# RWKV-7 scan of a hybrid trunk: the identity product of the state, cut to 64 rows and issued behind U

## The chip, the cores and the metric

The kernel runs on one core of a Trainium2 chip. The metric is the device time of one execution in microseconds (us), the median of several runs. An execution that the hardware profiler recorded comes with it; all durations of single instructions below are from that one execution.

## The reference

A trunk of four layers over 512 latent tokens and 256 context tokens, 1024 wide: a convolution module, a bidirectional RWKV-7 mixer, attention, a second convolution module. The change lies in the RWKV-7 layer, in the scan over tokens. Each of the 16 heads keeps a state S of 64 x 64, and for each token

```python
sa  = einsum("bhvk,bhk->bhv", S, -kk_t)
S   = S * d_t[:, :, None, :] + sa[..., None] * (kk_t * a_t)[:, :, None, :] + v_t[..., None] * k_t[:, :, None, :]
out = einsum("bhvk,bhk->bhv", S, r_t)
```

It runs once forwards and once backwards over the tokens, and the two outputs are added.

## The kernel before, in words

The scan works on chunks of 64 tokens (C = 64), so that a chunk is a few small matrix products in place of 64 steps. The 16 heads are taken in eight pairs; a pair p fills the 128 partitions, head 0 on partitions 0 to 63 (slice A), head 1 on 64 to 127 (slice B). There are 12 chunks, so 12 steps i for each pair and direction d. A **round** below is one pair p with its 12 steps; there are eight rounds, one after the other.

One step of one direction, `scan` (lines 1330 to 1389), is a generator that is advanced in six pieces. The tile VT holds, for each head, the state or U on the head's own 64 partitions and the values of the chunk on the other 64.

1. Line 1350, the **c products**: `pc[own, 0] = GM^T VT`, one product for each head, with all 128 rows of VT. Behind it, line 1354, the **identity products** `pS[own] = ident[:, hc]^T VT`: 128 rows by 64 columns, of which the 64 rows of the other half meet zeros in the identity. They put the old state into the PSUM half pS, for the sum of line 1373. They stand in the steps 1 to 10 of a round (`0 < i < 11`).
2. ACT copies the c product to **Z** (line 1093 by way of `cpy`).
3. Line 1361, the **R S products** into the half pO of the same bank (own state times R, 64 x 64), and line 1364, the **U products** `pc[own, 1] = Tt^T Z` (64 x 64).
4. ACT copies U into VT, one copy for each head (**U copies**, `cpy("U", ...)`, line 1093). They overwrite the old state in VT.
5. Line 1370 adds U and values to pO; line 1373 adds them to pS.
6. ACT scales pS into the VT of the next chunk (**state copies**, line 1378), and ACT (line 1093) or DVE (line 1385) takes pO into the output O.

pO and pS are two halves of one PSUM bank, tile `o0` or `o1` by direction, one buffer each. So the first product that writes the tile in a step must wait until ACT or DVE has read the tile of the step before; in the steps 1 to 10 that is the identity product of line 1354.

The order on PE, ACT, DVE and GpSimd is the order in which the code issues. The two directions alternate, d = 0 and then d = 1 for each piece, and between the pieces a list of events (`side`, `stream`) issues the work of other stages: the features of the next quarters (pz line 1116, pc line 1126; DVE's sg line 1122 stands between them), the Gram matrices (pg line 1166, masked by DVE in line 1170), turns (pt line 1192), the values of the next pair (pv line 1231), the triangular inverse of the next pair (DVE, tm line 1269 and Ti line 1272, in turn), its 64-wide part (px lines 1301 and 1314) and the centring of the last pair's output (gm line 1400). In the last round the gate's projection (line 189) fills the places between the pieces instead.

A matmul of 32-bit floats appears in the profile as two records, so the two heads' products of one direction, called a **pair of products** here, are four records ("x4").

Of the kernel before, what the change touches and what calls it, by code (L numbers as in the profile page):

```python
# [45 lines left out]
    A=[64.18, 65.3143, 66.1364, 69.4498, 69.7397, 70.3889],  # L46
    B=[2.44, 4.09473, 7.27024, 8.71365, 9.3943, 9.83957],
# [31 lines left out]
class Trunk:  # L79
# [952 lines left out]
    def rwkv_scan(self, i, rk, cv, vproj):  # L1032
        nc, tc, I = self.nc, self.tc, self.I
# [29 lines left out]
        ident = self.ident  # L1063
        self.mask3 = self.mask.rearrange("p (g c) -> p g c", c=C).unsqueeze(1).to_broadcast([P, 3, 2, C])
        A, B = slice(0, 64), slice(64, 128)
# [24 lines left out]
        def cpy(key, k, out, in_):  # L1090
            e = OPT["E"][key][k]
            if e == "a":
                nc.scalar.activation(out, in_, AF.Copy)  # L1093
            elif e == "d":
                nc.vector.tensor_copy(out, in_)
            else:
                nc.gpsimd.tensor_scalar(out=out, in0=in_, scalar1=1.0, scalar2=0.0, op0=ALU.mult, op1=ALU.add)
# [235 lines left out]
        def scan(p, d, G):  # L1333


            if d == 0:
                G["O"] = late["s"].tile([P, TOK], F32, tag="O", name="O", bufs=2)
            O, Tt = G["O"], G["Tt"]
            for i in range(12):
                h, q = divmod(i, NQ)  # L1340
                assert (p, h) in vdone and (p, h, d) in gdone and (p, h) in idone
                VT, GM, AR, BKT = (G["VT", h], *(G[n, h, d] for n in ("GM", "AR", "BKT")))
                dc = G["DC", h, d][:, q:q + 1]
                hc = lambda hd: slice(hd * C, (hd + 1) * C)
                pc = late["c"][d][:, 0:2 * C].rearrange("p (n c) -> p n c", c=C)
                po = late["p"].tile([P, 2 * C], F32, tag=f"o{d}", name=f"o{d}")
                pO, pS = po[:, 0:C], po[:, C:]
                for hd, own, oth in ((0, A, B), (1, B, A)):
                    rows = oth if i == 0 else slice(0, P)
                    nc.tensor.matmul(pc[own, 0, :], GM[rows, 2 * hd, q, :], VT[rows, d, q, hc(hd)], start=True, stop=True)  # L1350

                if 0 < i < 11:
                    for hd, own in ((0, A), (1, B)):
                        nc.tensor.matmul(pS[own], ident[:, hc(hd)], VT[:, d, q, hc(hd)], start=True, stop=False)
                yield
                Z = late["s"].tile([P, C], F32, tag=f"Z{d}", name="Z", bufs=1)
                cpy("Z", d, Z, pc[:, 0, :])
                yield
                if i:
                    for hd, own in ((0, A), (1, B)):  # L1360
                        nc.tensor.matmul(pO[own], VT[own, d, q, hc(hd)], AR[own, 1, q, :], start=i == 11, stop=False)
                tu = (h * 2 + d) * NQ + q
                for own in (A, B):
                    nc.tensor.matmul(pc[own, 1, :], Tt[own, tu, :], Z[own], start=True, stop=True)  # L1364
                yield
                cpy("U", 2 * d, VT[A, d, q, 0:C], pc[A, 1, :])
                cpy("U", 2 * d + 1, VT[B, d, q, C:2 * C], pc[B, 1, :])
                yield
                for hd, own in ((0, A), (1, B)):
                    nc.tensor.matmul(pO[own], VT[:, d, q, hc(hd)], GM[:, 2 * hd + 1, q, :], start=i == 0, stop=i == 11)  # L1370
                if i < 11:
                    for hd, own in ((0, A), (1, B)):
                        nc.tensor.matmul(pS[own], BKT[:, q, hc(hd)], VT[:, d, q, hc(hd)], start=False, stop=True)  # L1373
                yield
                if i < 11:
                    h2, q2 = divmod(i + 1, NQ)
                    for hd, own in ((0, A), (1, B)):
                        nc.scalar.activation(G["VT", h2][own, d, q2, hc(hd)], pS[own], AF.Copy, scale=dc[own])  # L1378

                c0 = (i if d == 0 else (3 - i if i < 4 else 15 - i)) * C  # L1380
                oc = O[:, c0:c0 + C] if d == 0 else O[:, c0:c0 + C][:, ::-1]
                if i in (0, 1, 4, 5, 6, 7):
                    cpy("O", d, oc, pO)
                else:
                    nc.vector.tensor_tensor(out=oc, in0=pO, in1=oc, op=ALU.add)
                if i == 11:
                    sdone.add((p, d))
                yield
# [93 lines left out]
        with ExitStack() as man:  # L1482
# [11 lines left out]
            for w in range(6):  # L1494
                ev = next(X)
                for n in range(18):
                    v_steps(18 * w + n)
                    for t, g in ev:
                        if n <= t < n + 1:
                            next(g)  # L1500
            chain = {p: [named(scan(p, d, GS[p]), f"scan{p}") for d in range(2)] for p in range(NT)}
            for p in range(-1, NT + 1):
                ev = side(p)
# [590 lines left out]
```

## Time and profile before

| | us |
|---|---|
| median of 3 runs | 2457.43 (2450.3 to 2457.45) |
| the profiled execution's own time | 2465.75 |
| its span from first to last instruction | 2464.0 |
| its first and last c product (line 1350) start at | 870.5 and 1404.8 |
| stretch 870 to 1410: PE, DVE, ACT busy | 486, 330, 357 of 540 |

In the timeline a row is a start, a length, an engine, a line with its operation, output and inputs, and in brackets the time that the engine stood idle before it and what ended that; an idle time below about 0.16 us is not shown. PE's records overlap, since matmuls are pipelined: the distance from start to start is what a product takes of PE, and the length contains its way through the array.

### The profile page before, as it was taken

How to read it: one execution, taken by the hardware profiler on the slowest of the kernel's cores; microseconds unless marked ns; L12 is line 12 of the kernel's file. 1: busy time of each engine (PE TensorE's matmuls, PEld its weight loads, DVE VectorE, ACT ScalarE, POOL GpSimd, SP SyncE). 2: the span in 40 equal slices, each digit the busy share in tenths (PEclk: the TensorE clock that was granted, in tenths of full speed). 3: DMA queues.
4: the chain of work that ended last, by engine and by line, in shares of the span. 5: the costliest groups of instructions: out<-in, count | busy, mean ns of one | idle time of the engine just before them, and what ended most of it. 6: DMA issues, size and time to landing. Idle time of an engine off the chain costs nothing. (4 is left out here: it accounts for less than half of the span.)

```text
span 2464.0 us, 45546 instructions
## 1 busy us (share of the span) xinstructions
PE 2252.8 (91%) x17855; PEld 1785.8 (72%) x17855; DVE 1445.3 (59%) x2597; ACT 1102.4 (45%) x2642; POOL 509.8 (21%) x600
## 2 busy tenths in 40 slices
PE   7999978899988798898988999888999999989987
PEld 4677757577666677777766678887999889865545
DVE  4787774734463766666664343546455464667664
ACT  4222243324542266666667543456455454432232
POOL 0000002000101232232210014544454444410000
PEclk8999989998989889899898999999999999989999
DMA  8787633365665644444434381111111211314442
GB/s 273 229 239 216 176 105 120 108 211 171 190 177 183 175 115 118 106 120 124 116 77 127 122 242 52 53 35 52 52 52 52 61 61 52 95 26 131 122 125 81
DMA packets 358897, 304.41 MB, mean 124 GB/s; under 512 B 110755, under 2 KB 300315, under 8 KB 358683
## 3 DMA queue, kind: packets, MB, share of 16 engines
q1 hardware_dynamic: 358683, 301.51, 42.3%
q8 instruction: 141, 2.31, 0.4%
q14 instruction: 73, 0.60, 0.1%
HBM read 215.82 MB, written 57.77 MB: 111 GB/s over the span
## 5 line engine op out<-in xcount | busy, mean ns | idle before, releaser
L176 ACT ACTIVATE whi<-wraw 128x1024 fp32r<-128x1024 f32 x168 | 177.0, 1056 | 383.9 <-PE cps L189 157.9
L374 DVE SCALAR_TENSOR_TENSOR Y<-yp,VC,Y 128x783 f32<-128x783 f32 (+1 forms) x256 | 229.2, 908 | 7.7 <-ACT Y L367 3.1
L178 DVE TENSOR_TENSOR wlo<-wraw,whi 128x1024 fp32r<-128x1024 f32 x98 | 120.4, 1229 | 175.7 <-ACT whi L176 175.7
L178 POOL TENSOR_TENSOR wlo<-wraw,whi 128x1024 fp32r<-128x1024 f32 x70 | 168.3, 2407 | 186.3 <-ACT whi L176 178.2
L1847 PE MATMUL pj<-whi,hhi 128*128 128x256 f32 x640 | 181.9, 285 | 5.2 <-ACT junk L1856 3.6
L189 PE MATMUL cps<-hhi,whi 128*128 128x512 f32 x576 | 179.3, 367 | 2.9 <-ACT hhi L288 2.9
L1847 PE MATMUL pj<-wlo,hhi 128*128 128x256 f32 x640 | 181.3, 284 | 0.0
L1847 PE MATMUL pj<-whi,hlo 128*128 128x256 f32 x640 | 181.2, 284 | 0.0
L189 PE MATMUL cps<-hlo,whi 128*128 128x512 f32 (+1 forms) x576 | 176.3, 360 | 0.0
L189 PE MATMUL cps<-hhi,wlo 128*128 128x512 f32 x576 | 176.0, 360 | 0.0
L189 PEld LDWEIGHTS cps<-hhi,whi 128*128 128x128 f32 x576 | 96.4, 190 | 48.3 <-issue 18.6
L1847 PEld LDWEIGHTS pj<-whi,hhi 128*128 128x128 f32 x640 | 123.1, 192 | 6.5 <-ACT junk L1856 4.2
L189 PE MATMUL ops<-hhi,whi 128*128 128x512 f32 (+1 forms) x320 | 104.5, 368 | 24.7 <-ACT hhi L449 22.4
L1847 PEld LDWEIGHTS pj<-wlo,hhi 128*128 128x128 f32 x640 | 123.2, 193 | 0.7
L1847 PEld LDWEIGHTS pj<-whi,hlo 128*128 128x128 f32 x640 | 122.8, 192 | 0.1
L1378 ACT ACTIVATE VT<-o,DC 64x64 f32<-64x64 f32 x352 | 108.5, 308 | 26.7 <-PE o L1373 17.2
L189 PEld LDWEIGHTS cps<-hlo,whi 128*128 128x128 f32 x576 | 96.2, 189 | 28.3 <-issue 10.1
L189 PEld LDWEIGHTS cps<-hhi,wlo 128*128 128x128 f32 x576 | 95.5, 189 | 24.1 <-issue 6.7
L189 PE MATMUL ops<-hhi,wlo 128*128 128x512 f32 (+1 forms) x320 | 106.7, 364 | 3.0 <-POOL wlo L178 2.2
L1093 ACT ACTIVATE VT<-c 64x64 f32<-64x64 f32 x384 | 83.5, 217 | 57.7 <-PE c L1364 49.5
L189 PE MATMUL ops<-hlo,whi 128*128 128x512 f32 (+1 forms) x320 | 105.0, 357 | 0.0
L1272 DVE TENSOR_TENSOR Ti<-Ti,tm 96x31 f32<-96x31 f32 (+15 forms) x248 | 99.7, 402 | 7.3 <-POOL tm L1269 1.3
(347 smaller groups left out, 5717.6 us busy)
## 6 DMA issues: line engine op xcount, KB each, us to landing
mraw<-in_mod_w_dram SPq DMA_DIRECT2D x36, 1024.0 KB
wraw<-in_conv_w_in_dram SPq DMA_DIRECT2D x48, 512.0 KB
wraw<-in_attn_w_in_dram SPq DMA_DIRECT2D x48, 512.0 KB
X<-yp SPq DMA_DIRECT2D x128, 98.9 KB
mraw<-in_mod_w_dram SPq DMA_DIRECT2D x24, 512.0 KB
KR<-dF SPq DMA_DIRECT2D x24, 384.0 KB
F<-dF SPq DMA_DIRECT2D x24, 384.0 KB
X<-yp SPq DMA_DIRECT2D x128, 65.5 KB
```

The source lines that it names most:

```text
L176: nc.scalar.activation(hi[:, :n], raw[:, :n], AF.Copy)
L178: lo_eng.tensor_tensor(out=lo[:, :n], in0=raw[:, :n], in1=hi.bitcast(F32)[:, :n], op=ALU.subtract)
L189: nc.tensor.matmul(ps, a[:, k, m0:m0 + m], b[k0 + k][:, ts], start=first and k == 0 and i == 0, stop=last and k == kt - 1 and i == 2)
L374: taps.append(lambda v=v: nc.vector.scalar_tensor_tensor(out=Y[m], in0=y[:, pe + v:pe + v + nout], scalar=self.vec("dw", nv)[:, v * NT + m ...
L1093: nc.scalar.activation(out, in_, AF.Copy)
L1272: eng("ia", j).tensor_tensor(out=Ti[0:96, j + 1:32, 0:c], in0=Ti[0:96, j + 1:32, 0:c], in1=o, op=ALU.add)
L1378: nc.scalar.activation(G["VT", h2][own, d, q2, hc(hd)], pS[own], AF.Copy, scale=dc[own])
L1847: nc.tensor.matmul(o[:, n, :], a, b[:, k, :], start=kh == 0 and k == 0 and e == 0 and n == 0, stop=kh == 1 and k == 3 and e == 2 and n == 1)
```

## The change

The identity products move from behind the c products to behind the U products, and use only the 64 rows of the head's own half: `ident[own, hc]` and `VT[own, ...]` in place of all 128 rows. So they are 64 x 64 products in a group of 64 x 64 products. In the steps 1 to 10 the R S product of line 1361 (1358 after the change) now writes the bank first and opens it (`start=True`), and the identity product adds with `start=False`. What is computed is the same, and so is the number of products: 20 pairs of products in a round.

```diff
                     nc.tensor.matmul(pc[own, 0, :], GM[rows, 2 * hd, q, :], VT[rows, d, q, hc(hd)], start=True, stop=True)
-
-                if 0 < i < 11:
-                    for hd, own in ((0, A), (1, B)):
-                        nc.tensor.matmul(pS[own], ident[:, hc(hd)], VT[:, d, q, hc(hd)], start=True, stop=False)
                 yield
                 Z = late["s"].tile([P, C], F32, tag=f"Z{d}", name="Z", bufs=1)
                 cpy("Z", d, Z, pc[:, 0, :])
                 yield
+
                 if i:
                     for hd, own in ((0, A), (1, B)):
-                        nc.tensor.matmul(pO[own], VT[own, d, q, hc(hd)], AR[own, 1, q, :], start=i == 11, stop=False)
+                        nc.tensor.matmul(pO[own], VT[own, d, q, hc(hd)], AR[own, 1, q, :], start=True, stop=False)
                 tu = (h * 2 + d) * NQ + q
                 for own in (A, B):
                     nc.tensor.matmul(pc[own, 1, :], Tt[own, tu, :], Z[own], start=True, stop=True)
+                if 0 < i < 11:
+                    for hd, own in ((0, A), (1, B)):
+                        nc.tensor.matmul(pS[own], ident[own, hc(hd)], VT[own, d, q, hc(hd)], start=False, stop=False)
                 yield
                 cpy("U", 2 * d, VT[A, d, q, 0:C], pc[A, 1, :])
```

PE's order in step 10 of a round, before (c is the tile of Z and U, o that of output and state, each with one number for each direction; `o<-VT,C` is the identity product, since C holds the identity; px and pt are work of other stages):

```order
L1350 MATMUL c_6692<-VT,GM 64x64 x2
L1354 MATMUL o_10002<-VT,C 64x64 x2
L1350 MATMUL c_6693<-VT,GM 64x64 x2
L1354 MATMUL o_10009<-VT,C 64x64 x2
L1301 MATMUL px<-TP,LO 32x32 x24
L1361 MATMUL o_10002<-AR,VT 64x64 x2
L1364 MATMUL c_6692<-Z,Tt 64x64 x2
L1361 MATMUL o_10009<-AR,VT 64x64 x2
L1364 MATMUL c_6693<-Z,Tt 64x64 x2
L1192 MATMUL pt<-C,BK 128x128 x3
```

PE's order at the same place after the change (lines 1358, 1361 and 1364 are now the R S, the U and the identity products):

```order
L1350 MATMUL c_6692<-VT,GM 64x64 x2
L1350 MATMUL c_6693<-VT,GM 64x64 x2
L1301 MATMUL px<-TP,LO 32x32 x24
L1358 MATMUL o_10002<-AR,VT 64x64 x2
L1361 MATMUL c_6692<-Z,Tt 64x64 x2
L1364 MATMUL o_10002<-VT,C 64x64 x2
L1358 MATMUL o_10007<-AR,VT 64x64 x2
L1361 MATMUL c_6693<-Z,Tt 64x64 x2
L1364 MATMUL o_10007<-VT,C 64x64 x2
L1192 MATMUL pt<-C,BK 128x128 x3
```

Two pairs of products have gone from ahead of px, one of them from between the two directions' c products, to a place ahead of pt, each right behind its direction's U products. The neighbours of both groups are the same as before.

ACT's order with its waits, before, at step 2 of a round (the four `VT<-c` are the U copies, two for each direction; `waits PE` is a wait for a product):

```order
L1093 ACTIVATE BKT<-pt 128x384
L1130 ACTIVATE Dt<-pc 128x6x64 [waits PE_49,Pool_49]
L1093 ACTIVATE VT<-c_6692 64x64 [waits PE_49,Activation_49]
L1093 ACTIVATE VT<-c_6692 64x64 [waits Activation_49]
L1093 ACTIVATE VT<-c_6693 64x64 [waits PE_49,Activation_49]
L1093 ACTIVATE VT<-c_6693 64x64 [waits Activation_49]
L1378 ACTIVATE VT<-o_12481,DC 64x64 [waits PE_49]
```

ACT's order at the same place after the change:

```order
L1093 ACTIVATE BKT<-pt 128x384
L1130 ACTIVATE Dt<-pc 128x6x64 [waits PE_49,Pool_49]
L1093 ACTIVATE VT<-c_6692 64x64 [waits PE_49,Activation_49] x2
L1093 ACTIVATE VT<-c_6693 64x64 [waits PE_49,Activation_49] x2
L1378 ACTIVATE VT<-o_12481,DC 64x64 [waits PE_49]
```

The order on ACT is the same, but each U copy now has its own wait for PE. A U copy overwrites the state that the identity product reads, and that product now stands behind the U product, so the copy waits for the identity product.

## The prediction

> **What bounds the kernel now.** I began with the head of the page and the table by stretches, to see how much of the span the scan has and who is busy in it.
>
> ```profile
> span 2464.0 us, 45546 instructions
> 870.00:1410.00 540.00, 485.93 (x7223) 381.73 (x7220) 330.21 (x808) 356.97 (x1296) 114.90 (x153) 0.92 0.44 113
> ```
>
> The steps that the change touches lie between 870 and 1410 us, 540 of 2464 us. PE is busy for 485.93 us of them, 90%, DVE for 330.21 (61%), ACT for 356.97 (66%). No engine is full, so time is lost in waits that pass from engine to engine, and what a product more or less costs depends on its place. Next I asked for the identity products themselves and for the waits of this stretch.
>
> ```profile
> L1354 PE MATMUL o<-VT,C x640: 222/222/368, 877.9 to 1397.4; 128*64 128x64 f32 x160
>   DVE O L1385: 12.8, 17
> ACT VT L1093 <- PE c L1364: 49.5, 61, 2.2
> PEld o L1370 <- ACT VT L1093: 19.3, 68, 1.1
> PEld c L1364 <- ACT Z L1093: 8.8, 15, 2.0
> ACT VT L1093 <- DVE VT L1095: 29.5, 27, 2.3
> ```
>
> The 640 records are 160 pairs of products (80 steps, two directions). In front of them PE and its weight loads stood idle for 12.8 us in all, waiting for DVE to take the old output out of the bank: what the change can remove at most, by this row. The next three rows are the chain that it touches at its new place: ACT waits 61 times for the U products, PE 68 times for the U copies, PE 15 times for Z. The last row, ACT copies of values that wait for DVE, matters in steps 5 and 6.
>
> **What a pair of products takes, by its place.** A step where the pairs stand close together, on PE alone:
>
> ```profile
> 1057.83 0.34 PE L1350 MATMUL c<-VT,GM 128*64 128x64 f32 x4
> 1057.99 0.29 PE L1354 MATMUL o<-VT,C 128*64 128x64 f32 x4
> 1058.11 0.29 PE L1350 MATMUL c<-VT,GM 128*64 128x64 f32 x4
> 1058.22 0.31 PE L1354 MATMUL o<-VT,C 128*64 128x64 f32 x4
> 1058.46 0.33 PE L1361 MATMUL o<-AR,VT 64*64 64x64 f32 x4
> 1058.63 0.28 PE L1364 MATMUL c<-Z,Tt 64*64 64x64 f32 x4
> 1058.74 0.28 PE L1361 MATMUL o<-AR,VT 64*64 64x64 f32 x4
> 1058.86 0.28 PE L1364 MATMUL c<-Z,Tt 64*64 64x64 f32 x4
> ```
>
> Starts inside a group are 0.11 to 0.12 us apart, with 128 rows (1057.99, 1058.11, 1058.22) as with 64 (1058.63, 1058.74, 1058.86). So a pair costs PE 0.12 us before and after, and the cut from 128 rows to 64 is worth nothing by itself. Going from the 128-row group to the 64-row one takes 0.24 (1058.22 to 1058.46); the number of such changes of form stays as it is, because the c products remain a 128-row group without the identity. What is left is the place. In each of the 80 steps two pairs, 0.23 us, leave the time before U and go behind it. Three things follow: (a) what stands behind the c products starts up to 0.23 earlier; (b) the U copies of a direction wait for one pair more, 0.12, and behind them on ACT wait the state copies and other stages' copies, on PE the products of line 1370; (c) what stands on PE behind the U products starts up to 0.23 later, less what (a) gave. Where PE never waits in between, (a) pays for (c). Where PE waits in between for something that does not come earlier, (a) is lost and (c) remains. So I went through the steps of one round in the middle, 1138 to 1204 us, by the timeline.
>
> **Steps 1 and 2.**
>
> ```profile
> 1145.63 0.33 PE L1364 MATMUL c<-Z,Tt 64*64 64x64 f32 x4 [0.24 <-ACT Z L1093]
> 1146.13 0.70 PE L1400 MATMUL gm<-O,C 128*128 128x256 f32 x2
> 1147.86 0.49 ACT L1120 ACTIVATE sg<-pz 128x384 f32<-128x384 f32 x1 [0.84 <-PE pz L1116]
> 1150.23 0.34 PE L1354 MATMUL o<-VT,C 128*64 128x64 f32 x4
> 1150.50 0.70 PE L1400 MATMUL gm<-O,C 128*128 128x256 f32 x2
> ```
>
> In step 1 PE waits for Z ahead of the U products, so starting that group earlier brings nothing, and gm, pt and pz behind it come 0.23 later; ACT already waits for pz, so this reaches the next step: +0.23. In step 2 the identity pair at 1150.23 stands directly ahead of gm, itself late because it waits for the bank. Without it gm and pc come up to 0.27 (1150.23 to 1150.50) earlier; I take 0.2. The U copies give 0.12 back: -0.1.
>
> **Steps 3 and 4.** Here stands the largest wait that goes.
>
> ```profile
> 1151.20:1163.20 12.00, 10.56 (x151) 7.58 (x150) 11.52 (x31) 7.86 (x31) 2.49 (x5) 1.00 0.32 100
> 1160.45 0.34 PE L1354 MATMUL o<-VT,C 128*64 128x64 f32 x4 [0.59 <-DVE O L1385]
> 1162.60 1.01 DVE L1170 TENSOR_TENSOR GM<-pg,C 128x384 f32<-128x384 f32 x2
> 1163.20 0.94 PE L1116 MATMUL pz<-RW,T 128*128 128x128 f32 x6 [0.22 <-DVE GM L1170]
> ```
>
> The identity pair waits 0.59 us for DVE, and pg and the U products behind it with it. After the change pg starts about 0.7 earlier. But DVE (third busy column) is busy for 11.52 of these 12.00 us with the inverse; it takes up GM when its own queue gets there, and pz waits for GM. So pz stays where it is, its wait grows from 0.22 to about 0.6, and the round gains nothing. The same cover takes the 0.12 of the U copies in step 3, which would otherwise cost that much: 0 for both steps.
>
> **Steps 5 and 6.**
>
> ```profile
> 1167.20 0.94 PE L1126 MATMUL pc<-C,sg 128*128 128x128 f32 x6 [0.44 <-DVE sg L1122]
> 1171.21 0.55 PE L1231 MATMUL pv<-C,V 128*128 128x128 f32 x3 [0.27 <-ACT VT L1093]
> 1175.53 0.63 PE L1231 MATMUL pv<-C,V 128*128 128x128 f32 x4 [1.42 <-ACT VT L1093]
> ```
>
> pc waits for DVE, so (a) is lost, and 0.23 appears behind U; but 0.27 us of PE's idle time ahead of pv takes it up, and in step 6 there is 1.42 of it. Both are waits for ACT's copies of values, which themselves wait for DVE (the 29.5 us above). So 0; without this cover it would be +0.23 each.
>
> **Steps 7 to 10.** DVE has no more inverse to do, and PE and ACT hand each other the chain.
>
> ```profile
> 1179.91 0.48 ACT L1093 ACTIVATE Z<-c 128x64 f32<-128x64 f32 x2 [0.33 <-PE c L1350]
> 1180.31 0.28 PE L1364 MATMUL c<-Z,Tt 64*64 64x64 f32 x4
> 1184.38 0.34 PE L1354 MATMUL o<-VT,C 128*64 128x64 f32 x4
> 1184.65 0.94 PE L1126 MATMUL pc<-C,sg 128*128 128x128 f32 x6
> 1189.44 0.46 ACT L1093 ACTIVATE Z<-c 128x64 f32<-128x64 f32 x2 [0.37 <-PE c L1350]
> 1189.82 0.28 PE L1364 MATMUL c<-Z,Tt 64*64 64x64 f32 x4
> 1193.54 0.95 PE L1301 MATMUL px<-TP,LO 32*32 32x32 f32 x48 [0.34 <-ACT VT L1093]
> 1196.68 1.31 ACT L1378 ACTIVATE VT<-o,DC 64x64 f32<-64x64 f32 x4 [0.76 <-PE o L1373]
> ```
>
> In step 7 the first Z is done at about 1180.15 (half of 0.48 after 1179.91) and U starts at 1180.31; less some 0.05 for the handing over, U can come 0.11 earlier, not 0.23: +0.12 for what stands behind. Step 9 likewise: Z done at 1189.67, U at 1189.82, so 0.1 earlier and +0.13. In step 8 the identity pair at 1184.38 stands alone ahead of pc; pc comes about 0.2 earlier, and with 0.23 behind U there remains +0.03. In step 10 px waits 0.34 for ACT, (a) is lost, and ACT's state copies already wait 0.76 for PE behind U: +0.23.
>
> **The last round** has the gate's products between the pieces, and PE is nearly full:
>
> ```profile
> 1345.00:1404.00 59.00, 56.00 (x489) 38.52 (x488) 17.92 (x24) 37.50 (x105) 0.61 (x1) 0.90 0.38 120
> ```
>
> With 56.00 of 59.00 us busy and the same pairs at the same price, only in other places: 0.
>
> **The sum.** A round: 0.23 - 0.1 + 0 + 0 + 0.12 + 0.03 + 0.13 + 0.23 = 0.64 us. Seven such rounds: +4.5 us. The profiled execution took 2465.75 us, so 2470.2 by its own time. The median of the runs is 8.3 us (0.34%) below it; on that scale 2457.43 + 4.5 = 2461.9, 0.18% more than before. A measurement of this kernel can tell about 0.3%, 7.4 us, from no change; so I expect none that can be told, with a lean to slower. The unknown costs: that all 12.8 us of idle time come back, -12.8; that 0.12 stays in every step, 80 x 0.12 = +9.6; that 0.23 does, +18.4.
>
> A rule against the change: the Trainium skill, "TensorE: Matmul & The Clock Gate", in the section on the per-tile semaphore tail, says that the signals of products that end together are written one after the other, 26.3 ns each. By the waits on ACT the U copies of a direction waited for one signal and now wait for two; taken for each of the 61 waits for U, an estimate from this page adds 61 x 0.026 = 1.6 us, and the sum would be 2463.5. No run here shows it yet.
>
> **Rivals.** First, slower: the chain Z, U, identity, U copy is the path in most steps, and what I took for cover is not. The point is whether DVE and the ACT copies behind it have slack against the state copies; from there each step pays 0.12 to 0.23. For it: ACT waits for U 61 times, 49.5 us. Against it: the 96% of DVE in steps 3 and 4. Price 9.6 to 18.4 us, 2467 to 2476.
>
> Second, faster: the 12.8 us of waiting for DVE come back whole, because GM, brought forward with pg, is taken up sooner than I think or because the removal reaches the state copies by another way. For it: the wait is real and on PE, which is 90% busy. Against it: pz. 2457.4 - 12.8 = 2444.6.
>
> Third, that the move changes nothing at all, since equal pairs only change places and PE waits elsewhere: 2457.4. The equal starts of 0.12 us speak for it, the Z waits in steps 1, 7 and 9 against it.
>
> **How the numbers follow.** My forecast 0.47, the first rival 0.26, the second 0.14, the third 0.13. The forecast's own range is -2 to +10 us, with step 2 and the absorbed steps the least sure; a little of it lies beyond 7.4 us. So slower by over 0.3%: 0.29; within: 0.56; faster: 0.15. The range reaches into both rivals, from 9.4 us below to 15.6 above: 2448 to 2473; what it leaves out is most of the second rival and the top of the first.
>
> **What would show it.** In the profile after: the identity products stand with no wait for DVE in front of them; pairs in the 64-row group start 0.12 apart; the U copies come 0.12 later after U; pz in step 4 waits longer for GM than 0.22 and starts no earlier against the step before; state copies in step 10 come later. Wrong would be: pz earlier with pg (then the second rival), or steps 3 to 6 longer by 0.12 or more each (then the first), or a pair at its new place costing other than 0.12.

## The result, and the profile after

| | before | after |
|---|---|---|
| median of 21 runs each, us | 2457.45 (2446.9 to 2466.2) | 2470.97 (2459.6 to 2488.0) |
| ratio of after to before | | 1.0062 (95% interval 1.0047 to 1.0077) |
| profiled execution: own time, span | 2465.75, 2464.0 | 2470.26, 2468.4 |
| mean granted clock of TensorE over the runs (before's: the 32 beside the first experiments) | 0.9534 | 0.9464 |

By the ratio the kernel became slower by 15.2 us (11.5 to 18.9); the two medians lie 13.5 apart. The forecast was +4.5, no difference that can be told; the measured time lies inside the range given, but among the prices of the first rival (2467 to 2476). The two profiled executions differ by only 4.5 us, because that of before was 8.3 us above its own median; the section on the clock comes back to this.

The whole scan of after, first c product to last, by the table of stretches:

```profile
865.40:1406.10 540.70, 474.59 (x7171) 371.75 (x7170) 326.13 (x803) 354.44 (x1290) 115.66 (x154) 0.91 0.44 112
```

In 540.70 us PE is busy for 474.59, and the granted clock (third from the right) is 0.91. The identity products themselves (line 1364 after the change):

```profile
L1364 PE MATMUL o<-VT,C x640: 218/218/311, 871.6 to 1401.2; 64*64 64x64 f32 x160
```

The waits of after, with the idle time in us, the times it happened and the longest:

```profile
ACT VT L1093 <- PE o L1364: 42.2, 59, 1.7
PEld c L1361 <- ACT Z L1093: 18.6, 22, 2.4
PE c L1361 <- ACT Z L1093: 15.3, 20, 2.2
PEld pz L1116 <- DVE GM L1170: 8.6, 6, 3.5
```

And three rows of before that belong beside them:

```profile
PEld o L1354 <- DVE O L1385: 7.1, 9, 1.9
PE o L1354 <- DVE O L1385: 5.7, 8, 1.8
PE c L1364 <- ACT Z L1093: 6.7, 15, 1.8
```

No wait for DVE is listed for the identity products any more; the R S products, which now open the bank, wait 0.7 us for DVE's copies of O. What went is less than 12.8 us: that figure adds the 7.1 of the weight loads (PEld) to the 5.7 of the products (PE), and in eight of the nine places both stood idle at the same time, so it was about 7 us of time. ACT's U copies now wait for the identity products (42.2 us). But PE's weight loads wait 18.6 us for Z where they waited 8.8 before, and the products behind them 15.3 where it was 6.7: nobody had touched Z. Two places of the timeline show new waits. First, step 3 of round 3, after (SPq rows are DMA issues on SP's queue):

```profile
1089.48 0.38 SPq L1112 DMA_DIRECT2D KR<-dF  x1
1090.10 0.26 SPq L1419 DMA_DIRECT2D dvar<-osq  x1
1092.59 0.42 ACT L1408 ACTIVATE osq<-O 128x256 f32<-128x256 f32 x1 [2.51 <-DMA dvar<-osq]
1093.28 0.33 ACT L1093 ACTIVATE Z<-c 128x64 f32<-128x64 f32 x2
1093.55 0.33 PE L1361 MATMUL c<-Z,Tt 64*64 64x64 f32 x4 [2.07 <-ACT Z L1093]
```

The same step before, in round 4:

```profile
1155.08 0.24 SPq L1419 DMA_DIRECT2D dvar<-osq  x1
1155.37 0.38 SPq L1112 DMA_DIRECT2D KR<-dF  x1
1156.99 0.33 ACT L1093 ACTIVATE Z<-c 128x64 f32<-128x64 f32 x2
1157.26 0.33 PE L1364 MATMUL c<-Z,Tt 64*64 64x64 f32 x4 [0.40 <-ACT Z L1093]
```

On SP the load of KR (features of a later pair, 384 KB) has moved ahead of the store of dvar (2x256 values, variances of the last pair's output, kept in the tile osq). osq has one buffer, so ACT's square of line 1408, which writes it next, waits until that store has landed, 2.49 us after its issue; Z stands behind the square on ACT and U behind Z on PE. The order on SP is not written by hand in this stretch, as that of the four other engines is; the scheduler chooses it. KR came out ahead in rounds 1, 2, 3 and 5 of after; in round 4 the store stayed ahead.

Second, step 8, after and then before:

```profile
1122.73 0.90 POOL L1143 TENSOR_TENSOR AR<-KR,Dt 128x384 f32<-128x384 f32 x1
1122.81 1.04 DVE L1095 COPY V<-Vr 128x384 f32<-128x384 f32 x1
1123.77 0.16 DVE L1138 COPY DC<-Dt 128x6 f32<-128x6 f32 x1
1124.00 0.63 PE L1231 MATMUL pv<-C,V 128*128 128x128 f32 x4 [0.84 <-DVE DC L1138]
```

```profile
1187.04 0.42 DVE L1095 COPY V<-Vr 128x384 f32<-128x384 f32 x1
1187.20 1.02 POOL L1143 TENSOR_TENSOR AR<-KR,Dt 128x384 f32<-128x384 f32 x1
1187.61 0.63 PE L1231 MATMUL pv<-C,V 128*128 128x128 f32 x4
```

Counted from the step's start, pc comes about 0.25 us earlier (0.2 was forecast), and so do Dt (decays, on ACT) and GpSimd's product AR (features times decays). AR now starts 0.08 us ahead of DVE's copy of V instead of 0.16 behind it, and the copy takes 1.04 us instead of 0.42. pv waits 0.84 us for DVE, which takes up the copy of DC behind that of V. In round 2 of after AR happened to start late:

```profile
1052.78 0.47 DVE L1095 COPY V<-Vr 128x384 f32<-128x384 f32 x1
1053.00 1.02 POOL L1143 TENSOR_TENSOR AR<-KR,Dt 128x384 f32<-128x384 f32 x1
1053.40 0.63 PE L1231 MATMUL pv<-C,V 128*128 128x128 f32 x4 [0.28 <-DVE V L1095]
```

There the copy took 0.47 us, and step 8 took 5.63 us where it took 6.20 in rounds 1 and 3.

To compare steps I took the time from a step's first c product to the next step's, out of the timeline. The traces show TensorE's clock granted in full or by half (below), so the table takes rounds 1 to 4 and of them only steps without half clock (for step 7, also none in step 6), and gives the median in us; only the range with KR ahead takes in round 5 too. Steps 5 and 6 are left out, because what one of them gains the next ones give back: step 6 alone lies anywhere from 4.49 to 6.60 us in the two profiles of after. Steps 5 to 7 together, where all three have the full clock, take 17.51 and 17.60 us before, and 17.49 and 17.58 after. The names are those of the experiments.

| step | 1 | 2 | 3 | 4 | 7 | 8 | 9 | 10 |
|---|---|---|---|---|---|---|---|---|
| before (two profiles) | 4.40 | 6.27 | 4.44 | 6.17 | 4.91 | 5.59 | 3.42 | 5.77 |
| after (two profiles) | 4.64 | 6.11 | 4.54 (5.79 to 5.93 with KR ahead) | 5.93 | 4.89 | 6.20 | 3.46 | 6.12 |
| e2_pinned | 4.63 | 6.12 | 4.53 | 5.95 | 4.88 | 6.20 | 3.46 | 6.12 |
| e3_osq2 | 4.63 | 6.12 | 3.56 | 7.19 | 4.88 | 6.20 | 3.46 | 6.08 |
| e4_ahead_pinned | 4.53 | 6.14 | 4.44 | 6.01 | 4.89 | 6.21 | 3.37 | 6.10 |
| e6_cut_alone | 4.40 | 6.27 | 4.43 | 6.18 | 4.77 | 5.60 | 3.70 | 5.77 |
| e7_move_pinned | 5.08 | 6.42 | 4.81 | 5.79 | 4.79 | 6.21 | 3.82 | 6.65 |
| e8_old8_10_pinned | 4.63 | 6.11 | 4.55 | 6.09 | 4.86 | 5.59 | 3.46 | 5.90 |

### The profile page after: what moved, and what is told of

It is laid out like the page before. It is cut to its first block, busy times and chain, and to the rows that moved or that the text cites. A ratio compares the mean times of both kernels' runs of the same rounds, so it can differ in the third digit from the quotient of the medians.

```text
span 2468.4 us, 45616 instructions
## 1 busy us (share of the span) xinstructions
PE 2244.3 (91%) x17855; PEld 1777.1 (72%) x17855; DVE 1442.7 (58%) x2597; ACT 1102.3 (45%) x2642; POOL 510.2 (21%) x600
## 3 DMA queue, kind: packets, MB, share of 16 engines
q1 hardware_dynamic: 358683, 301.51, 42.2%
## 5 line engine op out<-in xcount | busy, mean ns | idle before, releaser
L1093 ACT ACTIVATE VT<-c 64x64 f32<-64x64 f32 x384 | 83.5, 217 | 59.4 <-PE o L1364 42.2
```

## The experiments

Each was timed beside the kernel before on the same chip; there were four chips, one for e1 to e4, one for e5 to e8, one for e9 to e11 and one for e12. "Clock" is the mean granted clock of its runs. "Pinned" means that SP's order is held as in e2_pinned, "filled" that unread products fill PE's waits.

| kernel | ratio to before | clock, its own and before's |
|---|---|---|
| e1_after_again | 1.0045 (1.0026 to 1.0064) | 0.9479, 0.9534 |
| e2_pinned | 1.0041 (1.0021 to 1.0060) | 0.9454, 0.9534 |
| e3_osq2 | 1.0013 (0.9993 to 1.0034) | 0.9503, 0.9534 |
| e4_ahead_pinned | 1.0036 (1.0020 to 1.0053) | 0.9496, 0.9534 |
| e5_before_again | 1.0003 (0.9980 to 1.0027) | 0.9536, 0.9537 |
| e6_cut_alone | 1.0047 (1.0028 to 1.0066) | 0.9474, 0.9537 |
| e7_move_pinned | 1.0128 (1.0104 to 1.0153) | 0.9408, 0.9537 |
| e8_old8_10_pinned | 1.0031 (1.0009 to 1.0053) | 0.9464, 0.9537 |
| e9_before_filled | 0.9988 (0.9972 to 1.0005) | 0.9561, 0.9518 |
| e10_pinned_filled | 1.0012 (0.9998 to 1.0027) | 0.9539, 0.9518 |
| e11_old8_10_filled | 0.9979 (0.9960 to 0.9999) | 0.9553, 0.9518 |
| e12_new2_4_filled | 0.9976 (0.9961 to 0.9991) | 0.9548, 0.9535 |

**Again, unchanged: e1_after_again.** The change as it is.

> The changed kernel once more, on the same chip as the next three. Theory (DMA order): in rounds 1, 2, 3 and 5 the load of KR is issued on SP ahead of the small store of dvar, ACT's square waits for that store, Z stands behind it and U behind Z; step 3 of these rounds is 1.3 to 2.1 us longer than before, in round 4 it is not. With the pairs behind U this gives 1.004 to 1.008 of the kernel before, and the profile shows the long step 3 in the same four rounds again. Rival (the pairs behind U alone): 1.004 to 1.008 too, but the long steps fall on other rounds in this profile, as chance would have them.

The ratio came out within the error of the first (1.0045 against 1.0062), and the long step 3 stood in the same rounds 1, 2, 3 and 5, by 1.45 to 2.05 us against before (1.45 at full clock, the others partly at half). So the order on SP is a property of this kernel, and the step times repeat.

**The order on SP: e2_pinned.** The load of KR is held behind the first store of dvar of the round (shortened).

```diff
+            with tc.issue_after(first["dvar"]):
                 for o, t0, w in pieces(h, d):
                     nc.sync.dma_start(KR[:, :, o:o + w], ...)
```

> The changed kernel with one edge more in the issue order: the load of KR stays behind the round's first store of dvar on SP, as it stood before the change. Theory (DMA order): step 3 is again as long as before the change plus at most 0.2 us in all rounds, about 5.5 us less than the changed kernel (four rounds of 1.4 us net), 1.002 to 1.005 of the kernel before. Rival (the pairs behind U alone): within 1.5 us of the changed kernel, 1.005 to 1.007.

Step 3 of round 3, where the square again waits for the store, but only 1.25 us:

```profile
1082.89 0.24 SPq L1421 DMA_DIRECT2D dvar<-osq  x1
1083.18 0.38 SPq L1114 DMA_DIRECT2D KR<-dF  x1
1084.12 0.42 ACT L1410 ACTIVATE osq<-O 128x256 f32<-128x256 f32 x1 [1.25 <-DMA dvar<-osq]
1085.09 0.33 PE L1363 MATMUL c<-Z,Tt 64*64 64x64 f32 x4 [0.81 <-ACT Z L1094]
```

Step 3 is 4.53 to 4.55 us in rounds 1 to 5, 0.09 above before's. The cause of the long step 3 is thus shown: 1.3 to 1.4 us at full clock (rounds 3 and 5; in rounds 1 and 2 half clock adds to it), of which step 4 gave 0.1 back, in four rounds about 5 us. But the ratio, 1.0041, is only 0.0004 or 1 us below that of e1_after_again on the same chip, as the rival had it; the runs left something else open.

**The store's other end: e3_osq2.** A second buffer for osq, so that the square need not wait at all.

```diff
-                sq[t] = late["s"].tile([P, n], F32, tag="osq", name="osq")
+                sq[t] = late["s"].tile([P, n], F32, tag="osq", name="osq", bufs=2)
```

> The changed kernel with two buffers for osq, so that ACT's square no longer waits for the store of dvar; the order of the DMAs stays as the change has it. Theory (DMA order): the 2 us waits of the U products for Z in step 3 go although the store still lands late; 5 us or more less than the changed kernel, 1.000 to 1.004 of the kernel before. Rival (the pairs behind U alone): within 1.5 us of the changed kernel.

Step 3 became 3.56 us, 0.88 shorter than before's, and step 4 became 7.19, 1.02 longer. The pz row in step 4 says why:

```profile
1091.44 0.94 PE L1116 MATMUL pz<-RW,T 128*128 128x128 f32 x6 [1.35 <-DVE GM L1170]
```

pz waits 1.35 us for GM, 0.22 before. What PE gains in step 3 it waits for DVE in step 4; the prediction's cover holds, here for a gain that I had not forecast. Steps 3 and 4 together are 10.75 us, 0.27 above e2_pinned's, and yet this kernel's ratio is 0.0028 lower, 7 us. Its clock is higher, 0.9503 against 0.9454, which the section on the clock takes up.

**Identity ahead of U: e4_ahead_pinned.** The 64-row products stand between R S and U, with SP's order pinned.

> The identity products (64 rows) between the R S and the U products of their direction, with the same edge on SP. They then run while PE waits for Z in steps 1, 3, 7 and 9, and the U copies wait for U alone. Theory (the waits for Z decide what a pair behind them costs): 2 to 4 us less than with the identity behind U and the same edge, 1.000 to 1.003 of the kernel before. Rival (a pair costs its 0.12 us at any place in this group, since PE or ACT is behind it anyway): within 1 us of that kernel.

Against before step 1 costs 0.13 instead of 0.23, step 3 nothing instead of 0.09, and step 9 is 0.05 below, so the U copies' longer wait is about 0.1 us in these steps. The theory's 2 to 4 us did not come: the ratio is 0.0005 or 1 us below e2_pinned's. Steps 8 and 10 keep their 0.6 and 0.33: they do not come from the place behind U, but from the place left.

**Before against itself: e5_before_again.**

> The kernel before, unchanged, against itself. It tells how far two sets of runs of one kernel differ and how far a step differs from one profiled execution to the next. Expected: ratio 1.000 within 0.002; steps 3, 8 and 10 of rounds 1 to 5 within 0.1 us of the first profiled execution, steps 5 to 7 with differences of up to 2 us of both signs that cancel; the V copy of step 8 takes 0.41 us; the scan from the first c product to the last takes 533.1 us within 2. Rival: the step times themselves vary so much between executions that the +0.6 us in step 8 and the +0.35 in step 10 of the changed kernel are chance; then step 8 differs here by a few tenths too.

The full-clock steps repeat to a few hundredths, so +0.61 in step 8 and +0.35 in step 10 are not chance. But the scan, from the first c product to the first of the last step, took 525.8 us and not 533.1. The difference stood in steps 0, 1, 6 and 11, by 0.9 to 2.3 us at a time, in both directions, and in the slow ones the same PE products took longer: that is the clock.

**The cut alone: e6_cut_alone.** 64 rows at the old place, between the c products.

```diff
-                        nc.tensor.matmul(pS[own], ident[:, hc(hd)], VT[:, d, q, hc(hd)], start=True, stop=False)
+                        nc.tensor.matmul(pS[own], ident[own, hc(hd)], VT[own, d, q, hc(hd)], start=True, stop=False)
```

> The cut alone: the identity product has 64 rows but stands at its old place, between the 128-row c products. Theory: 64 rows are no cheaper than 128, and each change between 128-row and 64-row products costs 0.12 us more than the step inside a group, so a step with both directions together gets two more changes and becomes up to 0.24 us longer where PE decides (steps 7 to 10 and the last round): per round +0.3 to +1 us, in all +2 to +8 us, 2460 to 2466. V copy in step 8 at 0.41 us, step 3 unchanged since SP's order is that of before. Rival: the change of form costs nothing by itself (the 0.24 us was a wait), or two 64-row products run beside each other: no difference or up to 8 us faster, and the starts around L1354 stay 0.12 us apart.

Step 9, with the cut:

```profile
1119.18 0.34 PE L1350 MATMUL c<-VT,GM 128*64 128x64 f32 x4
1119.44 0.33 PE L1354 MATMUL o<-VT,C 64*64 64x64 f32 x4
1119.71 0.34 PE L1350 MATMUL c<-VT,GM 128*64 128x64 f32 x4
1119.97 0.33 PE L1354 MATMUL o<-VT,C 64*64 64x64 f32 x4
```

The starts are 0.26 us apart where they were 0.11 to 0.17. Going between 128 and 64 rows costs in both directions, and step 9 in rounds 0 to 5 and three steps of the last round are 0.28 longer. Elsewhere waits take it up. That is 9 x 0.28 = 2.5 us of the 11.5 measured, which is above the 2 to 8 expected. The rest stood in no step of the table; the clock of these runs was lower by 0.0063.

**The move alone: e7_move_pinned.** 128 rows at the new place, SP's order pinned.

> The move alone: the identity product keeps its 128 rows but stands behind U, and the store of dvar stays ahead of the load of KR on SP. Theory: against the kernel with the change and the same order on SP (ratio 1.0041) each step gets two or more changes of form between U and the copies, 0.12 us each, so steps 1, 7, 9 and 10 become 0.12 to 0.36 us longer: +0.5 to +1.2 us a round, +4 to +9 us in all, ratio 1.0055 to 1.0080. Step 8 keeps its +0.6. Rival: the form does not matter at all, and the place alone makes the time: ratio 1.004 and the same steps to 0.1 us.

Step 10, behind px:

```profile
1140.19 0.28 PE L1363 MATMUL c<-Z,Tt 64*64 64x64 f32 x4
1140.40 0.34 PE L1366 MATMUL o<-VT,C 128*64 128x64 f32 x4
1140.67 0.33 PE L1360 MATMUL o<-AR,VT 64*64 64x64 f32 x4
1140.83 0.46 ACT L1094 ACTIVATE VT<-c 64x64 f32<-64x64 f32 x2 [1.59 <-PE o L1366]
```

From a U pair past the identity to the next pair it takes 0.48 us (1140.19 to 1140.67) instead of 0.23 (in e2_pinned), the U copies wait for it, and steps 1, 9 and 10 are 0.68, 0.40 and 0.88 above before's, 0.45, 0.36 and 0.53 above e2_pinned's. It went the way that the theory said, but by more than it said, and step 7, which was to grow, did not. The clock is the lowest of all, 0.9408. So cut and move belong together: at the new place the cut saves some 0.9%, at the old one it costs 0.5%, the clock's share included in both.

**Steps 8 and 10 as before: e8_old8_10_pinned.** The new place in all other steps.

> The change everywhere but in steps 8 and 10, where the identity product stands at its old place with 128 rows; the store of dvar stays ahead of the load of KR on SP. Theory: in step 8 pc comes no earlier, GpSimd's product AR starts behind DVE's copy of V again, the copy takes 0.41 us and pv no longer waits for DC, so step 8 falls back to its old length (-0.6 us), and step 10 falls by 0.35: 0.95 us a round against the kernel with the change and the pinned order, some 5 to 6 us in all, ratio 0.9995 to 1.002. Rival: the V copy is slowed for another reason than the start of AR, or the time comes back in step 9 or 11: the scan keeps its 534 us and the ratio stays at 1.004.

Step 8, round 3:

```profile
1123.48 0.41 DVE L1096 COPY V<-Vr 128x384 f32<-128x384 f32 x1
1123.63 1.02 POOL L1145 TENSOR_TENSOR AR<-KR,Dt 128x384 f32<-128x384 f32 x1
1124.03 0.63 PE L1233 MATMUL pv<-C,V 128*128 128x128 f32 x4
```

The copy is first again and takes 0.41; step 8 is 5.59 as before, step 10 is 5.90. The cause of step 8 is shown. Yet the ratio, 1.0031, stayed above what I expected: of the five or six us that should have gone only 2.5 did (from 1.0041), and the profiled scan had 128 us at half clock, more than the 91 and 68 of before. So the theory of steps alone fell, and the clock had to be looked at.

**The clock.** First the stretches of 3.41 us around the wait of step 11 in round 1 of before (e5_before_again; columns as in the tables of stretches above, the granted clock third from the right):

```profile
988.35:991.76 3.41, 1.30 (x58) 1.15 (x57) 2.48 (x3) 3.03 (x10) 3.12 (x5) 1.00 0.57 108
991.76:995.17 3.41, 3.41 (x29) 3.05 (x30) 0.05 (x1) 1.47 (x6) 0.62 (x1) 0.50 0.68 130
```

And in after, around a wait of 2.22 us for Z in step 3 of round 2:

```profile
1022.58 0.33 PE L1361 MATMUL c<-Z,Tt 64*64 64x64 f32 x4 [2.22 <-ACT Z L1093]
```

```profile
1020.56:1023.97 3.41, 1.39 (x30) 1.25 (x30) 3.27 (x9) 1.85 (x8) 0.00 (x0) 1.00 0.46 179
1023.97:1027.38 3.41, 3.41 (x29) 2.27 (x29) 2.15 (x7) 1.96 (x8) 0.00 (x0) 0.50 0.00 0
```

A window in which PE did little is followed by one at half clock. Over the scans of the 14 profiles, on the grid of 3.41 us on which the clock changes in them, I took each window at full clock and summed over the records of PE's products that start in it the columns that they stream, weighted by the rows they use out of 128. Of 135 windows below 1600 such columns 133 were followed by half clock, of 58 between 1600 and 1800 it was 21, of 1627 above it was 8. Without the weight by rows the sides mix: between 1600 and 2600 columns 95 of 177. The best single cut puts 31 of the 1820 windows on the wrong side with the weight and 66 without. So by this tally a product of few rows counts less, and the cut would take activity away where nothing is gained by it. How much less 64 rows count is not settled: at three quarters in place of a half it is 28. Whether a wait falls into one window or is split over two is luck of the phase: before's two scans, with 91 and 68 us at half clock, differ by 7.3 us. Those of after have 99 and 111.

The Trainium skill, "TensorE: Matmul & The Clock Gate", section "What's actually happening", has the windows of 3413 ns and the half rate, and the trace agrees (3.41 us, 0.50); the section "HAM oscillation" of that page of the Trainium skill asks for no gap over about 3.4 us, and here a gap of 2.2 us was enough.

What half clock costs: among the runs of one kernel, 0.01 of mean clock goes with 13.1 us (fitted inside each of the kernels' sets of runs, correlations -0.65 to -0.95). The profiled execution of before had 0.947, 0.0064 under the mean of its runs, which is 8.4 us, and it lay 8.3 above its median. That of after does not fit so well: 0.951 is 0.0046 above the mean, 6 us, and it lay only 0.7 below its median. By the same fit the 0.0070 that after has less is 9 us of its 15.2, an estimate, and 6 are left at equal clock; on one chip, e1_after_again beside before, it is 7 of 11. For e6_cut_alone it is 8 of 11.5, for e2_pinned 10 of 10, for e8_old8_10_pinned 9.5 of 7.6, and the 7 us between e2_pinned and e3_osq2 are 6 of clock. The cost depends on the place: in before and after, half clock in step 0 made that step up to 2.3 us longer, one window of it in steps 5 to 7 of rounds 1 to 4 made the three together 0 to 0.5 longer.

To test it I filled PE's waits with products that nobody reads. In before these are six ahead of pc in step 11, one in step 5 and four ahead of the third pv of a round, in step 6 (shortened):

```diff
+            if d == 1 and 4 * p + 2 * h >= 10:
+                for _ in range(1 if h else 6):
+                    nc.tensor.matmul(late["c"][0][:, P:2 * P], self.tri, self.tri, start=True, stop=True)
             for j in range(3):
                 nc.tensor.matmul(pc[:, j * P:(j + 1) * P], ...)
```

In the two kernels with the change it is six, two and three.

> The kernel before, with 64 products more whose result nobody reads (128x128 constants into columns 128 to 255 of the bank of c, which nothing else uses; the output stays the reference's): six ahead of pc in step 11, one ahead of pc in step 5, four ahead of the third pv of a round in step 6, where PE otherwise waits 2.1, 0.4 and 1.4 us. Theory: TensorE's granted clock falls to a half for 3.4 us or more behind each window of 3.4 us in which PE was busy for less than about 55 per cent; filled waits keep the clock up. Of the 68 and 91 us at half clock inside the scan in the two profiles of before, those behind steps 6 and 11 go, 30 us or more; at 0.3 us of time for each us at half clock the scan becomes 9 us shorter, ratio 0.995 to 0.998, although PE has 17 us more to do. Rival: the half clock comes and goes with something else (a clock of its own, the load of the whole chip); then as much of it stays, and the time is the same or, where the added products reach the end of the wait, up to 5 us longer.

> The kernel with the change and the store of dvar ahead of the load of KR (ratio 1.0041 without filling), with unread products of the same kind: six ahead of pc in step 11, two ahead of pc in step 5, three ahead of the third pv in step 6 (65 in all). Theory: at equal clock this kernel is no slower than before, and its 10 us come from more time at half clock behind the longer waits of PE in steps 4 to 6; filled, the half clock in rounds 0 to 5 falls from 41 us to under 20, and the ratio to before comes to 0.995 to 0.999. Rival: the 10 us are in the steps themselves; then the ratio stays at 1.003 to 1.006.

> The same filling in the kernel that has the change everywhere but in steps 8 and 10 (ratio 1.0031 without filling, its steps 4.9 us shorter than before's at equal clock). Theory: with the clock held up the shorter steps show: ratio 0.992 to 0.997, faster than the filled kernel before. Rival: the steps gain nothing; ratio equal to that of the other filled kernels or above.

Step 11 of round 3, first in e5_before_again, then filled in e9_before_filled:

```profile
1122.46 0.91 PE L1126 MATMUL pc<-C,sg 128*128 128x128 f32 x6 [2.11 <-DVE sg L1122]
```

```profile
1120.30 1.60 PE L1127 MATMUL c<-C 128*128 128x128 f32 x12 [0.46 <-ACT Z L1093]
1121.96 0.91 PE L1129 MATMUL pc<-C,sg 128*128 128x128 f32 x6
```

The stretches of e9_before_filled around it:

```profile
1118.52:1121.93 3.41, 2.93 (x69) 2.56 (x69) 2.48 (x3) 3.07 (x10) 3.12 (x5) 1.00 0.62 115
1121.93:1125.34 3.41, 3.24 (x42) 2.79 (x42) 0.64 (x3) 1.75 (x6) 1.62 (x3) 1.00 0.48 87
```

The window has 2.93 us of work, where the one of round 1 further above had 1.30, and the next one has the full clock. (In round 3 of e5_before_again the wait of 2.11 us was split over two windows, and no half clock followed it either.) From step 9 of a round to step 2 of the next no half clock was left from round 0 to round 5 in any of the three filled kernels (44.4 and 13.7 us in the two profiles of before), and in rounds 0 to 5 it fell from 63.6 and 30.7 to 8.2 us, from 41.0 to 15.6 and from 73.6 to 15.4. The mean clock over the runs rose above before's in all three. So the mechanism is as the theory has it, and I had its size too large: all three ratios lie above what I expected, and the fillers of steps 5 and 6 make steps 5 to 7 together 0.2 to 0.5 us longer at full clock. But all three fell with more work on PE, by 0.0029 (pinned), by 0.0052 (old 8 and 10), and by 0.0012 for before, whose interval reaches past 1. That is 7, 13 and 3 us, where the fit gives 13, 14 and 6 for the clock regained, before what the fillers cost.

Between the filled kernels, pinned stands 0.0024 or 5.9 us above before. The table's +0.92 in each of six rounds gives 5.5, but the two clocks still differ by 0.0022, 3 us by the fit, so that the two agree is no proof of the steps. Old 8 and 10 stands 0.0009 below before, inside the intervals. The 4.9 us that its expectation took its steps to be shorter do not come out of the table, which gives +0.22 a round; steps 5 to 7 of e8_old8_10_pinned together are 17.48 us in the one of rounds 1 to 4 that has the full clock there, much as in the others. So no shorter steps show in the traces.

**A version that is faster: e12_new2_4_filled.** The change only in steps 2 and 4, where it shortened the step, six fillers in step 11, two in step 6.

> The change only in steps 2 and 4, where the step at full clock was 0.15 and 0.25 us shorter with it; in all others the identity product stands at its old place with 128 rows. The store of dvar stays ahead of the load of KR, and 44 unread products (constants, result read by nobody, the output stays the reference's) fill PE's waits: six ahead of pc in step 11, two ahead of the third pv in step 6. Theory: at full clock a round is 0.4 us shorter than before's, 2 to 3 us in all, and with the clock held up in steps 11 and 6 the filled kernel before's gain comes on top without its cost in step 5: ratio 0.995 to 0.998. Rival: the gains of steps 2 and 4 are given back in the steps behind them (step 5 or 6 longer by as much), and the ratio is that of the filled kernel before, 0.9988, or 1.

2450.27 against 2458.38 us, 0.9976: faster than before. Step 2 was 6.12, as with the change; step 4 was 6.27 and not 5.93, so that gain did not carry over. Step 6 was partly at half clock in each of rounds 1 to 5, so the two fillers there did not hold the clock up. Of the difference the clock (0.9548 against 0.9535) explains 1.7 us of 5.9 by the fit; which edit brought the rest was not tried, and since the interval overlaps that of e9_before_filled, no gain of the change itself is shown.

## Why the prediction was right or wrong, step by step

- **A pair takes 0.12 us with 128 or 64 rows, the cut is worth nothing.** Right for starts inside a group (0.11 to 0.12 in e2_pinned's step 10 too). Wrong in "the cut from 128 rows to 64 is worth nothing by itself": at its old place it costs 0.28 in step 9 by the changes of form, which the prediction saw as unchanged only because it thought of cut and move together; and the clock of its runs is 0.0063 lower. That this is because 64 rows count less in the window fits the tally, and is argued, not shown.
- **Step 1, +0.23**: measured +0.24. **Step 2, -0.1**: -0.16. **Step 7, +0.12**: -0.02; at full clock in steps 6 and 7 U came 0.25 us earlier in the step than before (1.53 after its start in place of 1.78, in e2_pinned and after), not the 0.11 taken from Z's end. **Step 9, +0.13**: +0.04; there U came 0.11 earlier, as taken, and what stands behind it came 0.15 later, not 0.23. **Step 10, +0.23**: +0.35, since px waits 0.59 for ACT (e2_pinned) where it waited 0.34.
- **Steps 3 and 4, 0.** On the four hand-ordered engines right: +0.10 and -0.24, and pz waits longer for GM (0.49 in e2_pinned, 0.22 before), as the prediction said. What failed is that SP was not looked at. Its order is left to the scheduler, and with PE's new order the load of KR went ahead of the store of dvar: 1.3 to 1.4 us at full clock, in four rounds. No term of the sum held it; e2_pinned takes it away.
- **Steps 5 and 6, 0.** Right as far as they can be told: with step 7 they take 17.49 and 17.58 us, 17.51 and 17.60 before.
- **Step 8, +0.03**: +0.61. "pc comes about 0.2 earlier" was right (0.25); that DVE's copy and GpSimd's product would change places for it was missed. e8_old8_10_pinned undoes it.
- **The sum of 0.64 a round**: at full clock 0.92 without steps 5 and 6, and 1.3 to 1.4 more in four rounds, 11 us over rounds 0 to 5. The last two rounds are seldom at full clock and could not be taken apart; by the difference to the 6 us at equal clock they came out some 4 to 5 us shorter, where the prediction had 0 for the last. That is argued, not shown.
- **Waits of PE cost nothing where another engine is late.** This is the assumption that failed for the larger part. A longer wait ahead of pz or pc was covered and did not move the step, but a longer wait leaves less in its window, and windows with little were followed by half clock. The prediction quoted granted clocks of 0.90 and 1.00 in its stretches and gave them no term. 9 us of the 15 by the fit, 7 of 11 in e1_after_again; that filling the waits gives clock and time back was shown, how much of the 15 us it was is an estimate, and in which steps it arose is not shown.
- **The first rival**, the chain of Z, U, identity and U copy in most steps: its price of 9.6 to 18.4 us holds the result, its mechanism does not. Steps 4 and 7 did not grow, steps 3 and 9 by 0.09 and 0.04 (e2_pinned), and e4_ahead_pinned shows about 0.1 us of it in steps 1, 3 and 9. **The second**, all 12.8 us back: only steps 2 and 4 became shorter, 0.4 together. Its price was too high besides, since the row of 12.8 counts most waits twice, once for the weight load and once for the product; about 7 us was there to come back. **The rule on semaphore signals** that the prediction cites from the Trainium skill, "TensorE: Matmul & The Clock Gate", section "The cost: per-tile semaphore tail", 26.3 ns for each: no run separates it, and step 7, where the U copies have the second wait too, did not grow.
- **The range, 2448 to 2473.** That it holds the 2470.97 is luck. The forecast's own sum, 2461.9, lies 9 us lower, and the two largest causes, the clock and SP's order, are in no term of it and in no rival; the range was wide for other reasons.

## What to carry to other kernels

When an edit changes one engine's order, compare every engine's order and SP's too: two DMAs that changed places cost the steps at full clock about as much as all the products that were moved, some 5 us each. Count a longer wait of PE as a cost even under full cover, by asking what the window of 3.41 us around it still holds, and take the granted clock of every run beside its time before a difference of half a per cent is put down to instructions. Compare steps at equal clock, over two profiles at least.

## What the runs showed of the hardware that I had not expected

- TensorE's clock dropped to 0.50 for a window of 3.41 us after a window with only 1.3 to 1.4 us of products, and 133 of 135 windows with under 1600 columns, weighted by rows, were followed by it; counted without the rows, the windows were told apart worse (66 of 1820 wrong in place of 31). Products with no use but to fill a wait made a kernel faster: from 1.0031 of before (e8_old8_10_pinned) to 0.9979 (e11_old8_10_filled).
- A DVE copy of 128x384 took 0.41 us when it started ahead of GpSimd's product and 1.04 us when it started 0.08 us behind it. The Trainium skill, "SBUF — State Buffer", section "Who interferes with whom", says that when a DVE instruction in a two-port mode, which a copy can enter, meets GpSimd, the one that issues first holds the shared ports and the other waits. The trace agrees in direction, the copy ending 0.22 us behind the product; whether the copy was in that mode no run shows.
- The instruction that waited for a store of 2x256 values started 2.49 us after the store's issue with a load of 384 KB ahead of it (after), and 1.23 us with the load behind it (e2_pinned).
